# A hybrid decoder step: low-rank products kept in SBUF, four kinds of small work put elsewhere, and the last output tile taken whole

## The chip, the cores and the metric

The kernel runs on one core of a Trainium2 chip. The core has five engines with an instruction queue each: TensorE (PE in the profile; its weight loads are listed as PEld), VectorE (DVE), ScalarE (ACT), GpSimd (POOL) and SyncE (SP). Each takes its instructions in the order in which they were written to its queue; semaphores join the queues. Nearly all loads and stores are issued by SP. The metric is the time of one execution on the device, in microseconds (us), as the median of several runs.

## The reference

The step computes one layer for a prompt of 16 meta tokens and 1024 tokens, and for 8 samples of 4 new tokens each. A token has 2048 features. In short:

```python
h = rms_norm(x, norm_pre_g)
sq, sk, sv, sg, gq, gk, gv, gg, ga = split(h @ w_in)   # 8 x (1024 wide), ga is 16 wide
log_f = log_sigmoid(ga @ w_alpha + b_alpha) / 16       # decay of the gated linear attention
o_sb  = stick_breaking_attention(sq, sk, sv)           # 8 heads of 128; samples read paged keys and values
o_gla = gated_linear_attention(gq, gk, gv, log_f)      # 4 heads, key 128, value 256, state per sample
mixed = concat(o_sb * silu(sg), rms_norm(o_gla) * silu(gg))
y     = x + rms_norm(mixed @ w_out, norm_post_g)
```

`gq`, `gk` are 512 wide in all, `w_alpha` is 16 x 512. The outputs are y for prompt and samples, the new keys and values, and the final states. All data are float32. The kernel gets float32 accuracy from TensorE by splitting an operand into a rounded part and a rest, and by adding three products.

## The kernel before, in words

**Layout.** The normalized input is held transposed in SBUF, 16 tiles `hT0` to `hT15` of 128 features by 1072 tokens, each as a rounded part `hh` and a rest `hl`. A projection (`inproj`, L279) makes 128 output columns: eight weight blocks, each for three chunks of tokens (`CHUNKS`: 384, 384 and 304 columns), each chunk with two times three products (L289 to L291) into one of three PSUM banks (`acc`). After the last block each bank is emptied by an `evac` function on ACT.

**Weaving.** PE has most of the work, so everything else is woven in between. `Weaver` holds generators; `W.beat()` is called after each chunk of a weight block (six products) and advances them. `yield n` in a generator means: go on n beats later. So the beat is the unit in which small work is placed. The program text that results is then ordered for each engine by the framework's scheduler, which replays it on a model of the chip, takes the ready instruction that stands first in the text, and thereby fixes each queue's order. Parts marked `urgent()` are preferred. A "NoSync" dependency makes the scheduler put one instruction behind another on the queue and adds no wait on the chip.

**Stages, in order.** (1) Input, norm, transposes. (2) Eight attention heads: projections of v, k, q, and the attention itself woven in; at the same time DVE multiplies the paged keys of all samples with their queries (`z_feed`, L384), and pairs of `w_out` blocks are subtracted (`weight_forms`). (3) `low_rank` (L309): `ga` for all tokens, 32 rows (a rounded weight and a rest), 96 products. (4) Gate groups 0 to 2 (`gate_group`, L435): projection of 128 gate columns, then `gate_rest` (SiLU times the attention output, stored to DRAM as `md`). (5) Four linear-attention heads g: projections gk, gq, gv; the generator `decay` (L715) builds the running sums of log_f from `ga`; `inside` the products within a chunk; `chunks` the recurrence over nine chunks. (6) Gate groups 5 to 13, and the samples' attention over pages (`chain`, `new_keys`, `paged_values`). (7) Gate groups 14 and 15. (8) The output projection: seven products of half-size matrices (`forms` 1 to 7) instead of eight, whose sums make the four quadrants of the result; then norms and stores, tile by tile.

**What the change touches.**
`low_rank` writes its three row groups (rounded part, rest, rounded part again) through SBUF staging tiles to the DRAM tile `gad` with nine stores (L326). `decay` loads for each head a piece of `w_alpha` six times over 96 rows (`walr`, L719) and for each chunk of tokens a piece of `gad` (L725), makes `wal` from it on ACT (L730) and DVE (L731), and multiplies (L739).
`packed` (L852) transposes 96 columns, and `by_token` (L862) transposes whole 128-column blocks, both into the same PSUM bank (tag `tr`, one buffer), which ACT (L857, L872) and for `packed` also DVE (L859) empty. In `inside` the packed keys come first and then the three `by_token` groups; in `gv_tok` the packed values follow the last `by_token` at once.
`new_keys` (L1101) sums the new keys with a matmul (`Cs`, L1104) on beat 10 of stage 6. `chain` (L1115) loads stored logits (`dz`, L1121) and adds a bias 3 beats later (L1123).
`early` and `later` (L1221, L1227) load quarters of `md` and subtract or add them 2 beats later.
`form` (L1273) casts an operand into rounded part (ACT, L1263) and rest (DVE, L1264) in the memory of old `hT` tiles; form 2 is needed by the second product of the output projection.
At the end, four tiles t = 0 to 3 of 128 rows get their last product (form 4, weights `kept`, L1478 to L1480, 24 products of 512 columns); `take_last` adds, squares and scales, and `finish1` makes the norm's factor and stores. The last tile t = 3 is done in two halves of 256 columns.

## Time and profile before

| what | value |
| --- | --- |
| median of 3 runs | 2122.7 us (2122.02 to 2126.62) |
| the profiled execution | 2123.69 us, its span 2122.0 us |
| mean granted TensorE clock | 0.994 of full speed |
| PE, DVE, ACT, POOL busy | 97%, 74%, 47%, 4% of the span |
| DMA | 304 MB, mean 143 GB/s |

The span is the time from the first to the last instruction of the program. A row of a timeline has start, duration, engine, line, operation and "out<-in" by the program's names; what stands in square brackets is the idle time of the engine just before, and what ended it. A row of the list of waits has the waiting instruction, what it waited for, the total in us, how often, and the longest. A row of sums over a stretch has the busy time and number of instructions of each engine, then PEclk, the granted clock of TensorE as a share of full speed. In the tables below "PE b" is a product of the output projection, "acc" one of a projection, "gx" the emptying of a gate group's bank.

### The profile page before, as it was taken

What the parts mean: (1) busy time and instruction counts of PE and PEld (TensorE: products, weight loads), DVE (VectorE), ACT (ScalarE), POOL (GpSimd) and SP (SyncE); (2) the same over time, 40 slices, a digit from 0 to 9 for tenths busy, and PEclk for the clock granted to TensorE, in tenths of its full rate; (3) what the DMA queues carried; (4) which work ended last, traced back from release to release, by engine and by line L of the source; (5) the groups of instructions that cost most, each with busy time, mean ns of one, the idle gap of its engine ahead of it and who ended that gap; (6) DMA issues with size and microseconds to landing.
All of it is one profiled execution on the core that took longest, in us unless ns stands there. A gap on an engine that the chain in (4) does not pass through costs nothing.

```text
span 2122.0 us, 43405 instructions
## 1 busy us (share of the span) xinstructions
PE 2062.5 (97%) x12570; PEld 1874.1 (88%) x12570; DVE 1574.2 (74%) x6596; ACT 995.4 (47%) x2538; POOL 81.1 (4%) x298
## 2 busy tenths in 40 slices
PE   5999999999999999999999999999999999999997
PEld 4999999999999989999898998998888897777776
DVE  6368888889888889899798898977544446453575
ACT  7345556565555556434435335353444335342342
POOL 0000000100001000100000000000000000000000
PEclk9999999999999999999999999999999999999999
DMA  6244443544444454553443444335777665352484
GB/s 199 72 100 126 130 128 103 141 127 114 135 129 122 110 140 117 157 139 116 114 130 109 132 122 126 101 81 156 233 231 239 219 198 188 129 159 71 131 286 173
DMA packets 380586, 304.02 MB, mean 143 GB/s; under 512 B 50426, under 2 KB 320954, under 8 KB 380346
## 3 DMA queue, kind: packets, MB, share of 16 engines
q1 hardware_dynamic: 378154, 300.97, 48.2%
q8 instruction: 99, 1.62, 0.3%
q14 instruction: 141, 1.16, 0.2%
q10 hardware_dynamic: 2192, 0.27, 0.1%
HBM read 243.39 MB, written 57.72 MB: 142 GB/s over the span
## 4 chain that ended last, share of the span: by engine, by line
PE 79%; DVE 8%; DMA 8%; ACT 2%; issue 2%; SPq 1%; POOL 0%; DVEq 0%; ACTq 0%; POOLq 0%
PE acc_g L289 4%; PE b L1478 4%; PE acc_g L291 4%; PE acc_g L290 4%; PE b L1479 4%; PE b L1480 4%; PE acc_k L289 3%; PE acc_k L290 3%; PE acc_k L291 3%; PE acc_q L289 3%; PE acc_q L290 3%; PE acc_q L291 3%; PE acc_gv L289 3%; PE acc_v L289 3%; PE acc_gv L290 2%; PE acc_gv L291 2%
## 5 line engine op out<-in xcount | busy, mean ns | idle before, releaser
L384 DVE SCALAR_TENSOR_TENSOR jk<-kp,qb 128x128 f32<-128x128 f32 x2048 | 590.5, 288 | 39.6 <-DMA qb<-qsd 2.2
L289 PE MATMUL acc_g<-hT,wh_g 128*128 128x368 f32 (+2 forms) x768 | 251.5, 327 | 1.2 <-ACT gx L438 1.1
L291 PE MATMUL acc_g<-hT,wl_g 128*128 128x368 f32 (+2 forms) x768 | 248.1, 323 | 0.0
L290 PE MATMUL acc_g<-hT,wh_g 128*128 128x368 f32 (+2 forms) x768 | 247.6, 322 | 0.0
L1478 PE MATMUL b<-ring,f 128*128 128x512 f32 x416 | 166.2, 401 | 7.0 <-ACT gx L438 3.6
L1314 DVE TENSOR_TENSOR ring<-wr,ring 128x512 fp32r<-128x512 f32 x104 | 70.9, 690 | 133.2 <-ACT ring L1313 133.0
L384 DVE DVE_READ_ACCUMULATOR jk<-kp,qb 128x1 f32 x2048 | 165.9, 81 | 0.0
L1479 PE MATMUL b<-ring,f 128*128 128x512 f32 x416 | 162.9, 392 | 0.4 <-DVE ring L1314 0.4
L1480 PE MATMUL b<-ring,f 128*128 128x512 f32 x416 | 162.6, 391 | 0.0
L289 PEld LDWEIGHTS acc_g<-hT,wh_g 128*128 128x128 f32 x768 | 144.7, 188 | 12.9 <-issue 7.3
L291 PEld LDWEIGHTS acc_g<-hT,wl_g 128*128 128x128 f32 x768 | 144.8, 189 | 2.0 <-issue 2.0
L290 PEld LDWEIGHTS acc_g<-hT,wh_g 128*128 128x128 f32 x768 | 144.9, 189 | 0.7
L1313 ACT CAST ring<-wr 128x512 fp32r<-128x512 f32 x104 | 64.4, 621 | 163.1 <-DMA wr<-in_w_out_dram 76.2
L289 PE MATMUL acc_gv<-hT,wh_gv 128*128 128x384 f32 (+1 forms) x384 | 129.2, 337 | 0.0
L289 PE MATMUL acc_k<-hT,wh_k 128*128 128x378 f32 (+1 forms) x384 | 127.6, 332 | 0.0
L290 PE MATMUL acc_k<-hT,wh_k 128*128 128x378 f32 (+1 forms) x384 | 125.4, 326 | 0.0
L289 PE MATMUL acc_q<-hT,wh_q 128*128 128x368 f32 (+2 forms) x384 | 125.3, 326 | 0.0
L291 PE MATMUL acc_gv<-hT,wl_gv 128*128 128x384 f32 (+1 forms) x384 | 125.3, 326 | 0.0
L291 PE MATMUL acc_k<-hT,wl_k 128*128 128x378 f32 (+1 forms) x384 | 125.2, 326 | 0.0
L290 PE MATMUL acc_gv<-hT,wh_gv 128*128 128x384 f32 (+1 forms) x384 | 124.7, 325 | 0.0
L290 PE MATMUL acc_q<-hT,wh_q 128*128 128x368 f32 (+2 forms) x384 | 123.6, 322 | 0.0
L291 PE MATMUL acc_q<-hT,wl_q 128*128 128x368 f32 (+2 forms) x384 | 123.5, 322 | 0.0
(440 smaller groups left out, 5414.5 us busy)
## 6 DMA issues: line engine op xcount, KB each, us to landing
kp<-in_cache_k_dram SPq DMA_DIRECT2D x512, 64.0 KB
vr<-in_cache_v_dram SPq DMA_DIRECT2D x64, 512.0 KB
tf<-in_w_out_dram SPq DMA_DIRECT2D x64, 256.0 KB
qb<-qsd SPq DMA_DIRECT2D x64, 256.0 KB
td<-tf SPq DMA_DIRECT2D x64, 256.0 KB
wr_g<-in_w_in_dram SPq DMA_DIRECT2D x128, 128.0 KB
wr<-td SPq DMA_DIRECT2D x64, 256.0 KB
wr<-in_w_out_dram SPq DMA_DIRECT2D x48, 256.0 KB
```

What stands on the lines that cost most here:

```text
L289: mm(acc[c][:, :n], wh[:, k2, :], hh[k][:, lo:hi], start=(k == 0), stop=False)
L290: mm(acc[c][:, :n], wh[:, k2, :], hl[k][:, lo:hi], start=False, stop=False)
L291: W.mark = mm(acc[c][:, :n], wl[:, k2, :], hh[k][:, lo:hi], start=False, stop=(k == NK - 1)).ins
L384: ins = vec.scalar_tensor_tensor(jk[:], kp[:], 1.0, qbs[h, b][:, t, :], ALU.mult, ALU.mult, accum_out=zt[:, t, NPG - 1 - i:NPG - i])
L1313: act.copy(wh, r)
L1314: vec.tensor_tensor(wl, r, wh.bitcast(F32), ALU.subtract)
L1478: mm(bk[:, cs], ah, wh, start=first and k == 0, stop=False, skip_group_check=True)
L1479: mm(bk[:, cs], ah, wl, start=False, stop=False, skip_group_check=True)
L1480: mm(bk[:, cs], al, wh, start=False, stop=last and k == 7, skip_group_check=True)
```

## The change

- The low-rank products stay in SBUF: a tile `ga` of 96 rows by 1072 tokens takes the three row groups straight from PSUM (two ACT copies and one DVE subtraction for each chunk). All of `w_alpha` is loaded once (`walr`). The DRAM tile, its 9 stores, the 12 loads of `ga` and the 4 loads of `walr` go; one load of `walr` comes. `decay` has no `yield 6` at its start any more.
- `low_rank` goes over four k at a time for one chunk, so the three chunks end one after another.
- Packed keys are transposed one beat behind the last `by_token` group; packed values one beat behind theirs.
- `new_keys` starts on beat 14 in place of 10; `chain` adds its bias 6 beats behind its load in place of 3; `early` and `later` add 5 beats behind theirs in place of 2.
- The ACT casts of form 2 get a NoSync dependency on the last `gx` of gate group 15.
- The last tile is done whole, as the other three.

```diff
+    ga = dk.tile([96, T], F32R, tag="ga", bufs=1, name="ga")
+    walr = dk.tile([96, GH * P], F32, tag="walr", bufs=1, name="walr")
     def low_rank_weights():
+        a = w_alpha[0]
+        nc.sync.dma_start(walr[:], bass.AP(tensor=a.tensor, offset=a.offset, ap=[[0, 6]] + [list(d) for d in a.ap]))
...
-        for k in range(NK):
+        for kb in range(0, NK, 4):
             for c, (lo, hi) in enumerate(CHUNKS):
                 n = hi - lo
-                mm(acc[c][:32, :n], wa[k // 8][:, k % 8, :], hh[k][:, lo:hi], start=(k == 0), stop=False)
-                mm(acc[c][:32, :n], wa[k // 8][:, k % 8, :], hl[k][:, lo:hi], start=False, stop=(k == NK - 1))
+                for k in range(kb, kb + 4):
+                    mm(acc[c][:32, :n], wa[k // 8][:, k % 8, :], hh[k][:, lo:hi], start=(k == 0), stop=False)
+                    mm(acc[c][:32, :n], wa[k // 8][:, k % 8, :], hl[k][:, lo:hi], start=False, stop=(k == NK - 1))
+                W.beat()
             W.beat()
...
-                act.copy(hi_[:, :n], acc[c][:32, :n])
-                vec.tensor_tensor(lo_[:, :n], acc[c][:32, :n], hi_[:, :n].bitcast(F32), ALU.subtract)
-                for i, t in enumerate((hi_, lo_, hi_)):
-                    nc.sync.dma_start(gad[32 * i:32 * i + 32, lo:hi], t[:, :n].bitcast(F32))
+                ps = acc[c][:32, :hi - lo]
+                act.copy(ga[0:32, lo:hi], ps)
+                act.copy(ga[64:96, lo:hi], ps)
+                vec.tensor_tensor(ga[32:64, lo:hi], ps, ga[0:32, lo:hi].bitcast(F32), ALU.subtract)
...
+    evacs = []
     def gate_group(g):
         def evac(c, ps, lo, hi):
             x = stage(f"gx{g}_{c}")
-            act.copy(x[:, :hi - lo], ps)
+            evacs.append(act.copy(x[:, :hi - lo], ps).ins)
...
         def decay(g, cb):
-            raw = stage(f"walr{g}")[:96, :P]
...
-            load_ga(0)
-            yield 6
+            gs = slice(g * P, (g + 1) * P)
+            raw = walr[:, gs]
             wal = gp.tile([96, P], F32R, tag="wal", name=f"wal{g}")
...
-                mm(ps[:, :n], wal[:], ga[:, :n], start=True, stop=True)
+                mm(ps[:, :n], wal[:], ga[:, lo:hi], start=True, stop=True)
...
-            packed(rep_, pk[:], 2, f"k{g}")
             by_token(kt, kd, (0, 4), col, f"k{g}")
             yield 1
             by_token(kt, kd, (4, 4), col, f"k{g}")
             yield 1
             by_token(kt, kd, (8, 1), col, f"k{g}")
             res["kd"], res["ebl"], res["pk"] = kd, ebl, pk
+            yield 1
+            packed(rep_, pk[:], 2, f"k{g}")
...
             if c == 2:
+                yield 1
                 packed(rep, pv[:, f * P:(f + 1) * P], 1, f"v{g}_{f}")
...
         def new_keys():
-            yield 10
+            yield 14
...
             nc.sync.dma_start(z[:].rearrange("p a r -> p (a r)"), zd[b][:])
-            yield 3
+            yield 6
...
         def early(k):
-            yield 2
+            yield 5
         def later(k):
-            yield 2
+            yield 5
...
-        def split(hi, lo, src):
-            act.copy(hi, src)
+        def split(hi, lo, src, behind=None):
+            ins = act.copy(hi, src)
+            if behind is not None:
+                tc.add_manual_dep(ins.ins, behind.name, NOSYNC, reason="behind")
...
-                    split(f[:, 0], f[:, 1], combined(p, k))
+                    split(f[:, 0], f[:, 1], combined(p, k), evacs[-1] if p == 2 else None)
...
         for t in range(4):
             tot = before_last(t)
-            w = 256 if t == 3 else 512
-            for f in range(512 // w):
-                for k in range(8):
-                    product(banks[t], t, 4, k, kept[k], False, True, slice(f * w, (f + 1) * w))
-                    W.beat()
-                take_last(t, banks[t], tot, f, w)
-            finish1(t, tot[:, 512 // w:512 // w + 1])
+            for k in range(8):
+                product(banks[t], t, 4, k, kept[k], False, True)
+                W.beat()
+            take_last(t, banks[t], tot)
+            finish1(t, tot[:, 1:2])
```

`finish1` itself is not edited: it still forms the last output of tile 3 in two halves of 256 columns, each with its own store.

More of the change, by code (lines that the diff above doesn't have):

```diff
@@ L151, in hybrid_step @@
     znd = dram.tile([NSMP, HEADS, NSMP], F32, name="znd")
-    gad = dram.tile([96, T], F32, name="gad")
     td = [dram.tile([P, 8, 1024], F32, name=f"td{j}") for j in range(4)]
@@ L295, in inproj @@
                 W.beat()
+    dk_cm = tc.tile_pool(name="dk", bufs=2, side="right")
+    dk = dk_cm.__enter__()
     wa = []
+    ga = dk.tile([96, T], F32R, tag="ga", bufs=1, name="ga")
+    walr = dk.tile([96, GH * P], F32, tag="walr", bufs=1, name="walr")
     def low_rank_weights():
+        a = w_alpha[0]
+        nc.sync.dma_start(walr[:], bass.AP(tensor=a.tensor, offset=a.offset, ap=[[0, 6]] + [list(d) for d in a.ap]))
         war = stage("war")
@@ L319, in low_rank @@
             with urgent():
-                n = hi - lo
-                hi_ = stg.tile([32, 384], F32R, tag="stg", name=f"gah{c}")
-                lo_ = stg.tile([32, 384], F32R, tag="stg", name=f"gal{c}")
-                act.copy(hi_[:, :n], acc[c][:32, :n])
-                vec.tensor_tensor(lo_[:, :n], acc[c][:32, :n], hi_[:, :n].bitcast(F32), ALU.subtract)
-                for i, t in enumerate((hi_, lo_, hi_)):
-                    nc.sync.dma_start(gad[32 * i:32 * i + 32, lo:hi], t[:, :n].bitcast(F32))
-    dk_cm = tc.tile_pool(name="dk", bufs=2, side="right")
-    dk = dk_cm.__enter__()
+                ps = acc[c][:32, :hi - lo]
+                act.copy(ga[0:32, lo:hi], ps)
+                act.copy(ga[64:96, lo:hi], ps)
+                vec.tensor_tensor(ga[32:64, lo:hi], ps, ga[0:32, lo:hi].bitcast(F32), ALU.subtract)
     paged = {}
@@ L715, in decay @@
         def decay(g, cb):
-            raw = stage(f"walr{g}")[:96, :P]
-            a = w_alpha[0, :, g * P:(g + 1) * P]
-            nc.sync.dma_start(raw, bass.AP(tensor=a.tensor, offset=a.offset, ap=[[0, 6]] + [list(d) for d in a.ap]))
-            gas = {}
-            def load_ga(c):
-                lo, hi = CHUNKS[c]
-                gas[c] = stg.tile([96, 384], F32R, tag="stg", name=f"ga{g}_{c}")
-                nc.sync.dma_start(gas[c][:, :hi - lo].bitcast(F32), gad[:, lo:hi])
-            load_ga(0)
-            yield 6
+            gs = slice(g * P, (g + 1) * P)
+            raw = walr[:, gs]
             wal = gp.tile([96, P], F32R, tag="wal", name=f"wal{g}")
@@ L734, in decay @@
                 yield 5
-                ga = gas.pop(c)
-                if c < 2:
-                    load_ga(c + 1)
                 ps = gps.tile([P, 512], F32, tag="P", bufs=2, name=f"al{g}_{c}")
-                mm(ps[:, :n], wal[:], ga[:, :n], start=True, stop=True)
+                mm(ps[:, :n], wal[:], ga[:, lo:hi], start=True, stop=True)
                 ny = stage(f"ny{g}_{c}")[:, :n]
@@ L1387, in before_last, with take_last @@
             return tot
-        def take_last(t, bk, tot, f, w):
-            cs = slice(f * w, (f + 1) * w)
+        def take_last(t, bk, tot):
             u = sums_[4 + t, 1]
-            if f == 0:
-                scaled[t] = raw(f"og{t}")
+            scaled[t] = raw(f"og{t}")
             with urgent():
-                vec.tensor_tensor(u[:, cs], bk[:, cs], u[:, cs], ALU.add)
-            part = ssq[:, 4 + t, 2 + f:3 + f]
-            act.activation(bk[:, cs], u[:, cs], AF.Square, accum_out=part)
-            vec.tensor_tensor(scaled[t][:, cs], u[:, cs], gains[1][:, cs], ALU.mult)
-            vec.scalar_tensor_tensor(tot[:, f + 1:f + 2], part, 1.0 / D, tot[:, f:f + 1], ALU.mult, ALU.add)
+                vec.tensor_tensor(u, bk[:], u, ALU.add)
+            part = ssq[:, 4 + t, 2:3]
+            act.activation(bk[:], u, AF.Square, accum_out=part)
+            vec.tensor_tensor(scaled[t][:], u, gains[1][:], ALU.mult)
+            vec.scalar_tensor_tensor(tot[:, 1:2], part, 1.0 / D, tot[:, 0:1], ALU.mult, ALU.add)
         def sample_y(sc, b):
@@ L1473, in finish1, with product @@
                     nc.sync.dma_start(y_prompt[0, 512 + i * P:512 + (i + 1) * P, ys], o[:, cs])
-        def product(bk, t, p, k, w, first, last, cs=slice(0, 512)):
-            wh, wl = (x[:, cs] for x in w)
+        def product(bk, t, p, k, w, first, last):
+            wh, wl = w
             ah, al = (forms[p, k][:, s_, t * P:(t + 1) * P] for s_ in range(2))
-            mm(bk[:, cs], ah, wh, start=first and k == 0, stop=False, skip_group_check=True)
-            mm(bk[:, cs], ah, wl, start=False, stop=False, skip_group_check=True)
-            mm(bk[:, cs], al, wh, start=False, stop=last and k == 7, skip_group_check=True)
+            mm(bk[:], ah, wh, start=first and k == 0, stop=False, skip_group_check=True)
+            mm(bk[:], ah, wl, start=False, stop=False, skip_group_check=True)
+            mm(bk[:], al, wh, start=False, stop=last and k == 7, skip_group_check=True)
         SB = {}
```

## The prediction

> **What bounds the kernel now.** I read the page's busy times first, then the list of what PE waited for, then sums over stretches behind those waits, and last the timelines around each wait that the change can touch.

> ```profile
> PE 2062.5 (97%) x12570; PEld 1874.1 (88%) x12570; DVE 1574.2 (74%) x6596; ACT 995.4 (47%) x2538; POOL 81.1 (4%) x298
> ```

> PE is busy for 97% of a span of 2122.0 us. The change takes no product away, so a gain can only come out of PE's idle time and out of what that idle time does to its clock. The list of waits says where that is (total, times, longest):

> ```profile
> PE al L739 <- DMA ga<-gad: 4.1, 2, 2.8
> PE b L1478 <- ACT gx L438: 3.6, 1, 3.6
> PE trp_v L856 <- ACT gv L872: 3.3, 3, 2.3
> PE Cs L1104 <- issue: 2.9, 1, 2.9
> PE tr_k L867 <- DVE pk L859: 2.2, 3, 0.7
> PE b L1478 <- ACT b L1398: 2.2, 1, 2.2
> PE acc_ga L315 <- DVE q L621: 1.6, 2, 1.5
> PE acc_g L289 <- ACT gx L438: 1.1, 1, 1.1
> PE otr L891 <- ACT gst L893: 0.7, 3, 0.2
> PE trp_k L856 <- DVE rep_k L850: 0.4, 1, 0.4
> ```

> Those of 2.2 us and more are each near an edit; the waits of the start, which no edit touches, are left out. What they cost beyond their length is in the granted clock (the eighth figure is PEclk) of the stretches behind them, in the order al, a later al, trp_v, Cs, b after gx, b after L1398:

> ```profile
> 896.00:900.00 4.00, 4.00 (x15) 4.00 (x16) 3.79 (x25) 1.61 (x3) 4.00 (x16) 0.60 0.39 112
> 911.00:915.00 4.00, 3.96 (x24) 3.96 (x25) 3.69 (x25) 1.54 (x6) 0.00 (x0) 1.00 0.56 175
> 1134.60:1140.00 5.40, 5.37 (x28) 5.38 (x29) 3.17 (x23) 2.32 (x8) 0.00 (x0) 0.68 0.32 97
> 1485.70:1491.00 5.30, 5.25 (x22) 4.65 (x23) 3.61 (x9) 2.16 (x5) 0.00 (x0) 0.68 0.65 226
> 1771.00:1775.00 4.00, 4.00 (x12) 3.14 (x13) 3.81 (x11) 4.00 (x10) 0.00 (x0) 0.62 0.17 30
> 2109.00:2113.00 4.00, 4.00 (x23) 4.00 (x24) 1.61 (x4) 0.00 (x0) 0.00 (x0) 0.63 0.62 240
> ```

> Each wait of 2.2 us or more is followed by a slow stretch; the second al wait (4.1 - 2.8 = 1.3 us) is not. A slow stretch loses (1 - PEclk) x length: 1.6, 1.7, 1.7, 1.5 and 1.5 us.
> [...] The rows show it after 2.2 us already, so I count it.

> **The change, part by part.**

> *Low-rank products in SBUF.* Both al waits go, since `ga` needs no load: 4.1 + 1.6 = 5.7 us. The 25 DMAs that go and the one that comes are issued by SP between waits and cost PE nothing. `walr` has an effect on another wait:

> ```profile
> 1133.54 0.30 ACT L730 CAST wal<-walr 96x128 fp32r<-96x128 f32 x1 [2.61 <-DMA walr<-in_w_alpha_dram]
> 1134.63 0.31 PE L856 MATMUL trp_v<-ident,rep_v 128*96 128x128 f32 x1 [2.25 <-ACT gv L872]
> ```

> ACT stands 2.61 us at the cast of `wal`, and behind it on its queue stands the copy that frees the transposes' bank; PE's 2.25 us at trp_v is the wait for that copy. With `walr` resident the cast waits for nothing, so the 3.3 us of trp_v go with this part, whatever the beat of `packed` is: 3.3 + 1.7 = 5.0 us. What is late next there is the copy itself, which the scheduler has counted.

> *Extra evacuation work and order in `low_rank`.* Three more ACT copies.

> ```profile
> 794.64 0.84 ACT L323 CAST gah<-acc_ga 32x384 fp32r<-32x384 f32 x2 [1.25 <-PE acc_ga L316]
> ```

> Two take 0.84 us, so three cost 1.3 us of an ACT that stood idle 1.25 us there; the first two chunks now end 16 and 8 products earlier and cover it. The 1.5 us wait at the start of `low_rank` is for the bank of chunk 0, needed first in both orders: it stays; the other 0.1 us goes. I take 0, ends -1.3 and +0.1. `decay` starts 6 beats earlier and so still meets the chunk recurrence: three otr waits of 0.2 us stand beside al products now; if all 9 al products of heads 1 to 3 met one, that would cost 9 x 0.2 = 1.8 less the 0.7 there. I take -0.5.

> *Transposes sharing a bank.*

> ```profile
> 992.35 0.66 PE L867 MATMUL tr_k<-ident,gk 128*128 128x128 f32 x4 [0.74 <-DVE pk L859]
> ```

> The packed keys hold the bank through an ACT and then a DVE step (pk), and the next user waits 0.74 us for it. With the packed keys last, that goes for tr_k (2.2 + 0.4 = 2.6 us at most), but the value transposes use the same bank in the same beats, and one of them will stand behind pk. The end +2.6 is no follower waiting, 0 the same wait moved, -2.6 the wait doubled. Nearest is the moved wait with a beat between: +1.0.

> *Key sums; bias; first forms' sums.* Between the start of gate group 5 and Cs, and up to a later load of `dz`, the projections' products are:

> ```profile
> 1464.00:1485.70 21.70, 18.75 (x116) 18.45 (x116) 0.39 (x1) 1.00 0.56 163
> 1464.00:1534.50 70.50, 60.55 (x360) 58.27 (x360) 3.05 (x7) 0.98 0.68 215
> 1534.55 0.34 SPq L1121 DMA_DIRECT2D dz<-zd  x1
> 1482.52 0.42 DVE L1123 TENSOR_TENSOR dz<-dz,bias 128x256 f32<-128x256 f32 x1 [1.53 <-DMA dz<-zd]
> 1485.25 0.41 DVE L1086 TENSOR_TENSOR spb<-spn,bmask 32x256 f32<-32x256 f32 x1
> ```

> A beat is six products, so Cs stands 116 / 6 = 19.3 beats in, while the text has it on beat 10: what placed it was its operand `spb`, ready in the scheduler's model only then. Beat 14 is ahead of 19.3 too. And the load of `dz` for batch 3 stands on beat 60, twelve ahead of its place in the text (72): work off PE runs as soon as it is ready, whatever its beat. So I expect nothing from 10 to 14, 3 to 6 and 2 to 5: 0. The upper end is the whole wait, 2.9 + 1.7 = 4.6 us; the lower, that the 1.1 us wait at gate group 15 (its ACT work stands behind DVE sums that wait for loads) doubles: -1.1.

> *Casts of form 2 behind gate 15.*

> ```profile
> 1763.91 0.62 ACT L1263 CAST f<-q 128x512 fp32r<-128x512 f32 x1 [2.43 <-DMA q<-md]
> 1766.98 0.30 PE L291 MATMUL acc_g<-hT,wl_g 128*128 128x304 f32 x1
> 1770.33 0.46 ACT L438 COPY gx<-acc_g 128x368 f32<-128x368 f32 x1
> 1772.12 0.40 ACT L438 COPY gx<-acc_g 128x304 f32<-128x304 f32 x1
> ```

> Eleven casts, six f<-q (form 2) and five f<-s (form 6), run on ACT from 1763.91 to 1770.33, 0.58 us apart, ahead of the gx that PE waits for. Only the f<-q are put behind. If the five others start at 1763.91 they end at 1763.91 + 5 x 0.58 = 1766.8, and gx at 1767.3, when PE's last product (1766.98 + 0.30) ends: 3.6 + 1.5 = 5.1 us go. Late next are the weights of blocks 6 and 7:

> ```profile
> 1784.80 1.54 SPq L1204 DMA_DIRECT2D small<-md  x1
> 1786.91 0.86 SPq L1312 DMA_DIRECT2D wr<-in_w_out_dram  x2
> 1791.71 0.50 PE L1478 MATMUL b<-ring,f 128*128 128x512 f32 x1 [0.62 <-ACT ring L1313]
> ```

> SP holds that load behind `small`, which reads gate 15's last store; that chain starts with the last gx, which moves from 1772.12 to the end of the products, some 1767.7: 4.4 us, where PE moves 5.1. So this wait grows by 0.7 us. The eight casts of form 2 now lie beside the gate's own work on ACT; one in its way costs 0.6. I take 5.1 - 0.7 - 0.6 = 3.8, ends 0 and 5.1.

> *Last tile whole.*

> ```profile
> 2098.18 0.39 PE L1478 MATMUL b<-keep,f 128*128 128x512 f32 x1
> 2103.62 0.28 PE L1478 MATMUL b<-keep,f 128*128 128x256 f32 x1
> 2104.36 0.68 DVE L1396 TENSOR_TENSOR u<-b,u 128x512 f32<-128x512 f32 x1
> 2107.14 0.75 DVE L1472 SCALAR_TENSOR_TENSOR u<-u,r_y,xrs 128x512 f32<-128x512 f32 x1
> 2116.38 1.41 DVE L1472 SCALAR_TENSOR_TENSOR y<-y,r_y,xr 128x512 f32<-128x512 f32 x2
> 2117.70 0.87 DVE L1472 SCALAR_TENSOR_TENSOR og<-og,r_y,xrs 128x256 f32<-128x256 f32 x2
> ```

> A whole tile takes 2103.62 - 2098.18 = 5.4 us, so the last ends at 2109.2. DVE gives tile 2's four outputs, two in 1.4 us, until 2107.14 + 2.7 = 2109.8, then adds; from add to first output 2.8 us (2107.14 - 2104.36), so 2112.6; the outputs take 2.9 (0.75 less overlap, 1.4, 0.87), so 2115.5; from there to the end of the span 2122.0 - 2118.6 = 3.4: 2118.9. Gain 3.1 us. The half tiles' overlap, which is given up, is in that count. Ends 1.0 (all longer steps twice in a row) and 3.8 (the add goes ahead of one 0.7 us output).

> **Sum.** 5.7 + 5.0 + 0 - 0.5 + 1.0 + 0 + 3.8 + 3.1 = 18.1 us, against the profiled execution's 2123.7 (span 2122.0): 2105.6. Its own time is 1.0 above the runs' median of 2122.7, so the median comes to 2104.6; I say 2105.

> **The rivals.**
> (a) *The key sums' wait goes too* (if DVE no longer stands 1.53 us at `dz` ahead of `spb`): 2105 - 4.6 = 2100.
> (b) *The weight blocks take back what form 2 gave.* A wait at a pair of blocks that reaches 2.2 us brings a slow stretch: 2.2 - 0.6 + 1.6 = 3.2 us a pair; at two pairs, with the 0.7 counted already, 2105 + 5.7 = 2111. For it: the wait is there (0.62) and grows; against: 0.7 more isn't 2.2.
> (c) *Slow stretches stay though waits go*, because something else than these waits sets them: 1.6 + 1.7 + 1.5 back, 2110. Against it: five of five waits of 2.2 us or more have one and the 1.3 us wait has none. [...]
> (d) *New order, same idle time.* The scheduler lays every queue anew; fresh waits as large as those removed: 2122.
> (e) *Slower:* SP starves the output projection. The second form's loads wait for buffers that its casts free, and the casts stand behind gx; if SP holds weight loads behind them, each pair of blocks costs 2.2 + 1.6 = 3.8 us. The rest gains 14.3, so four pairs even out; at five it is 2122.7 - 14.3 + 19 = 2127. Against it:

> ```profile
> SPq L1312 <- PE sc L1498: 8.9, 3, 6.2
> ```

> SP's weight loads wait for PE's own last reading of the old block, so they come earlier when PE does.

> **How the numbers follow.** Forecast 0.58, (a) 0.14, (b) 0.11, (c) 0.06, (d) 0.05, (e) 0.06. The range takes in (a), (b) and (c), and beside them some 2 us for the bank's ends: 2098 to 2113. Within 0.2% (4.2 us, about what a measurement can tell from no change) only (d): 0.05; slower (e) 0.06; faster 0.89.

> **What would show it.** No al, trp_v or b-after-L1398 wait and no half clock at those places; no ACT idle before `wal`; gx of gate 15 ending near PE's last product; Cs still waiting about 2.9 us with a slow stretch; a DVE wait before a transpose of values. Wrong: a Cs wait much longer (PE ahead of DVE), or waits over 2 us at L1478 in the first steps.

## The result, and the profile after

The changed kernel takes 2112.4 us (median of six runs, 2108.2 to 2114.1) where the kernel before takes 2122.8: a ratio of 0.9947, 95% interval 0.9934 to 0.9959, or 11.3 us (8.7 to 14.0) less. The forecast was 2105, its range 2098 to 2113, so the result is inside by 0.6 us. The profiled execution of the changed kernel took 2108.2 us, its span is 2106.5; it is the shortest of the six. The profile page has for it:

```profile
PE 2056.2 (98%) x12546; PEld 1868.4 (89%) x12546; DVE 1569.7 (75%) x6593; ACT 991.8 (47%) x2539; POOL 80.9 (4%) x298
```

PE is still the bound, with 24 products fewer because the last tile is no longer computed in two halves. The list of what PE waited for (line and what was waited for, then total, times, longest, in us; the start is left out):

```profile
PE Cs L1097 <- issue: 2.3, 1, 2.3
PE acc_gq L288 <- ACT gk L673: 2.2, 1, 2.2
PE b L1471 <- ACT b L1344: 2.0, 2, 1.2
PE acc_gk L288 <- ACT gx L442: 1.8, 1, 1.8
PE Us L961 <- DVE km L958: 1.5, 1, 1.5
PE acc_ga L321 <- DVE q L625: 1.3, 1, 1.3
PE acc_gq L288 <- ACT gk L680: 1.2, 1, 1.2
PE b L1471 <- ACT gx L442: 1.2, 1, 1.2
PE acc_g L288 <- ACT gx L442: 0.8, 1, 0.8
...
PE tr_v L859 <- DVE pk L851: 0.7, 1, 0.7
```

`al`, `trp_v`, `tr_k` and the 2.2 us wait for the first half of the last tile (b on L1398) are gone; one `tr_v` wait of 0.7 us behind `pk` has come, as forecast. The b wait for gx fell from 3.6 to 1.2, Cs kept 2.3. What no step of the forecast had are acc_gk, acc_gq (two) and Us: 1.8 + 2.2 + 1.2 + 1.5 = 6.7 us of new waits.

For all kernels below I added up PE's gaps of over 0.1 us between products from the trace, by stretch, and the time lost to half clock (half the length of those stretches up to PE's last product, since the granted clock is 0.50 in them; those after the last product cost nothing and are left out; the wait ahead of the first b product counts with the output projection):

| kernel | span | 870 to 1000 (first head) | 1000 to the last gv | last gv to 1495 | 1495 to first b | output projection | half clock |
|---|---|---|---|---|---|---|---|
| before | 2122.0 | 5.5 | 5.6 | 3.4 | 1.4 | 9.7 | 10.2 |
| changed | 2106.5 | 5.1 | 2.0 | 3.9 | 1.1 | 4.0 | 6.8 |
| changed, second trace | 2111.9 | 6.5 | 1.9 | 4.6 | 1.2 | 4.1 | 6.8 |

The second trace (an execution of 2113.6 us, near the median) is the one to set beside the kernel before: 10.1 us less span. The output projection gave 5.6, the heads after the first 3.7, the half clock 3.4; the first head gave nothing (+1.0) and the stretch up to Cs took 1.2 back. The end behind PE's last product is 0.9 us longer in both. Of the half clock, 3.4 us in the changed kernel's first trace and 1.7 in the other two lie ahead of 60 us; past 60 us it costs 8.5, 3.4 and 5.1 us in the three rows.

### The profile page after: what moved, and what is told of

Read it like the earlier page. It is cut to its first block, busy times and chain, and to the rows that moved or that the text cites. A ratio compares the mean times of both kernels' runs of the same rounds, so it can differ in the third digit from the quotient of the medians.

```text
span 2106.5 us, 43298 instructions
## 1 busy us (share of the span) xinstructions
PE 2056.2 (98%) x12546; PEld 1868.4 (89%) x12546; DVE 1569.7 (75%) x6593; ACT 991.8 (47%) x2539; POOL 80.9 (4%) x298
## 3 DMA queue, kind: packets, MB, share of 16 engines
q14 instruction: 142, 1.16, 0.2%
## 4 chain that ended last, share of the span: by engine, by line
PE 84%; DMA 6%; DVE 6%; ACT 2%; issue 1%; SPq 0%; DVEq 0%; POOL 0%; ACTq 0%; POOLq 0%
PE acc_g L288 4%; PE acc_g L290 4%; PE b L1471 4%; PE acc_g L289 4%; PE b L1472 4%; PE b L1473 4%; PE acc_k L288 3%; PE acc_gv L288 3%; PE acc_k L289 3%; PE acc_q L288 3%; PE acc_k L290 3%; PE acc_gv L290 3%; PE acc_gv L289 3%; PE acc_q L289 3%; PE acc_q L290 3%; PE acc_v L288 3%
## 5 line engine op out<-in xcount | busy, mean ns | idle before, releaser
L289 PE MATMUL acc_g<-hT,wh_g 128*128 128x368 f32 (+2 forms) x768 | 247.9, 323 | 0.0
L1472 PE MATMUL b<-ring,f 128*128 128x512 f32 x416 | 162.8, 391 | 0.7 <-DVE ring L1309 0.5
L288 PEld LDWEIGHTS acc_g<-hT,wh_g 128*128 128x128 f32 x768 | 145.1, 189 | 12.4 <-issue 10.2
L289 PEld LDWEIGHTS acc_g<-hT,wh_g 128*128 128x128 f32 x768 | 145.1, 189 | 0.7
L289 PE MATMUL acc_k<-hT,wh_k 128*128 128x378 f32 (+1 forms) x384 | 125.5, 327 | 0.0
L289 PE MATMUL acc_gv<-hT,wh_gv 128*128 128x384 f32 (+1 forms) x384 | 124.6, 325 | 0.0
L289 PE MATMUL acc_q<-hT,wh_q 128*128 128x368 f32 (+2 forms) x384 | 123.8, 322 | 0.0
```

The lines of the kernel that those rows point to most:

```text
L288: mm(acc[c][:, :n], wh[:, k2, :], hh[k][:, lo:hi], start=(k == 0), stop=False)
L289: mm(acc[c][:, :n], wh[:, k2, :], hl[k][:, lo:hi], start=False, stop=False)
L1472: mm(bk[:], ah, wl, start=False, stop=False, skip_group_check=True)
```

## The experiments

Each time below is set against runs of the kernel before that were made beside it on the same chip, as a ratio with its 95% interval; the microseconds are 1 less that ratio, times the median of those runs. Those medians differ (2126.4, 2122.7 and 2124.7 in three series of runs), so only ratios are compared from one series to another.

### One part at a time

**The low-rank part alone** (`lowrank`): `ga` and `walr` in SBUF, the sums in runs of four blocks, `decay` without loads and lag.

```diff
-            raw = stage(f"walr{g}")[:96, :P]
...
-            yield 6
+            gs = slice(g * P, (g + 1) * P)
+            raw = walr[:, gs]
...
-                mm(ps[:, :n], wal[:], ga[:, :n], start=True, stop=True)
+                mm(ps[:, :n], wal[:], ga[:, lo:hi], start=True, stop=True)
```

> The kernel before with the low-rank part alone: ga and walr in SBUF, the sums over 32 blocks in runs of four, decay without its loads and without its lag of six beats. The forecast's terms 5.7 + 5.0 - 0.5 give 10.2 us less than before, some 2112.6, with no al and no trp_v wait. Rival (earlier decay blocks ACT): in the changed kernel's trace PE waits 1.76 us for gx at the first acc_gk product and 2.16 + 1.19 us for gk at acc_gq, with a slow stretch of 1.7 us after them, because ACT stood 5.2 us at an exponential of the decay that now comes earlier; if the low-rank part makes these, they stand in this trace too and the gain is 10.2 - 6.3 = 4 us, some 2119.

Ratio 0.9981 (0.9970 to 0.9992): 4.0 us less (1.7 to 6.4). That is the rival's number; its cause, the earlier `decay`, is a part of it only, as the next kernel shows. PE's waits between 870 and 1000 us in this kernel:

```profile
PE acc_gq L288 <- ACT gk L678: 2.5, 1, 2.5
PE acc_gk L288 <- ACT gx L440: 2.4, 1, 2.4
PE acc_gq L288 <- ACT gk L671: 1.3, 1, 1.3
PE tr_k L856 <- DVE pk L848: 0.7, 1, 0.7
```

The two al waits are gone and three waits of 6.2 us in all stand in their place. So the new waits belong to this part and not to the others.

**Only `walr` resident** (`walr`); gad, its loads and the lag stay.

```diff
-            raw = stage(f"walr{g}")[:96, :P]
-            a = w_alpha[0, :, g * P:(g + 1) * P]
-            nc.sync.dma_start(raw, bass.AP(tensor=a.tensor, offset=a.offset, ap=[[0, 6]] + [list(d) for d in a.ap]))
+            raw = walr[:, g * P:(g + 1) * P]
```

> The kernel before with walr resident in SBUF alone; gad and its loads and the lag of six beats stay. The forecast takes the trp_v waits to be those of an ACT queue that stands at the wal cast for its load: then 3.3 + 1.7 = 5.0 us go, some 2117.7, and the al waits on ga stay at 4.1. Rival (the trp_v waits come from something else in the order of the queue, and went in the changed kernel by the transposes' new order): 2122.7, with trp_v still waiting.

Ratio 0.9992 (0.9982 to 1.0003): 1.7 us less (0.6 more to 3.8 less), so the 5.0 lie outside. In the same stretch:

```profile
PE acc_gk L289 <- ACT gx L441: 2.1, 1, 2.1
PE al L740 <- DMA ga<-gad: 1.8, 1, 1.8
PE al L740 <- DMA wr_gk<-in_w_in_dram: 0.8, 1, 0.8
...
PE trp_v L857 <- ACT gv L873: 0.4, 1, 0.4
```

Of 3.3 us of trp_v 0.4 is left, although `packed` stands where it stood: those waits were the `wal` cast's load, as argued. But acc_gk appears with this edit alone: it is in each of the seven traces with `walr` resident and the gates' order unchanged, and in none of the five without `walr`.

**The transposes' order alone** (`transp`), the two `yield 1` and `packed` last.

```diff
-            packed(rep_, pk[:], 2, f"k{g}")
...
             res["kd"], res["ebl"], res["pk"] = kd, ebl, pk
+            yield 1
+            packed(rep_, pk[:], 2, f"k{g}")
...
```

> The kernel before with the order of the transposes alone: the packed ones behind those by token. The forecast: 1.0 us less (ends: 2.6 less and 2.6 more), with the three tr_k waits of 0.74 us gone and a wait at a value transpose in their place. Rival (the trp_v wait of 2.25 us with its slow stretch moves too, since the packed value transposes now come a beat later): 3.9 us more go, 2118 or less. In the changed kernel's trace one tr_v wait of 0.69 us is left.

Ratio 0.9988 (0.9977 to 0.9998): 2.5 us less (0.4 to 4.9). The tr_k waits are gone; trp_v has three waits of 3.8 us in all, the longest 1.5, where before it had 3.3 with one of 2.25. The idle time of the heads after the first is 5.6 us in both traces; what is gone there is the half clock at 1135.7 (a granted clock of 0.51 from 1135.7 to 1139.1 us), which stood behind a single wait of 2.25 us and doesn't stand behind the three shorter ones. This is one trace of each; elsewhere in it, too, half clock is absent at places that the edit does not touch.

**The four yields alone** (`yields`).

```diff
-            yield 10
+            yield 14
...
```

> The kernel before with the four changed yields alone (10 to 14, 3 to 6, 2 to 5 twice). The forecast: 0 us, the wait at Cs stays at 2.9 us with its slow stretch (in the changed kernel 2.34 us and a slow stretch, after the same 19.3 beats). Rival: the page sums' later places make DVE free ahead of the key sums, Cs waits 1 us less and the stretch goes: 2.7 us less, 2120.

Ratio 0.9998 (0.9987 to 1.0009): nothing. Cs waits 3.0 us and is followed by half clock.

**Form 2's casts alone** (`casts`).

```diff
-                    split(f[:, 0], f[:, 1], combined(p, k))
+                    split(f[:, 0], f[:, 1], combined(p, k), evacs[-1] if p == 2 else None)
...
```

> The kernel before with form 2's casts behind gate 15's last gx alone. The forecast: 3.8 us less, some 2119, the weight blocks' wait of 0.62 us grows to about 1.3. Rival 1 (only the wait that the changed kernel's trace shows gone, 3.55 to 1.16, and no slow stretch): 2.4 + 1.5 = 3.9 and the ring waits of 0.62 + 0.22 go too: 4.7, some 2118. Rival 2 (SP holds weight loads behind the form's own loads): new waits above 1 us at the first weight blocks, 2122 or more.

Ratio 0.9986 (0.9977 to 0.9996): 3.0 us less (0.9 to 4.9). What is left of the wait is seen in the changed kernel's timelines of ACT and PE (start, length, what ran, idle time before it and what ended it):

```profile
1757.42 0.46 ACT L442 COPY gx<-acc_g 128x368 f32<-128x368 f32 x1
1758.30 0.48 ACT L442 COPY gx<-acc_g 128x384 f32<-128x384 f32 x1 [0.42 <-PE acc_g L290]
1760.38 0.92 ACT L427 ACTIVATE gs<-gs 128x368 f32<-128x368 f32 x2 [1.60 <-DVE gs L426]
1761.21 0.39 ACT L442 COPY gx<-acc_g 128x304 f32<-128x304 f32 x1
1761.66 0.49 PE L1471 MATMUL b<-ring,f 128*128 128x512 f32 x1 [1.16 <-ACT gx L442]
```

No cast stands ahead of the last gx any more. The gate's own exponential does, and it waits 1.60 us for DVE; PE waits 1.16 for the copy behind it. That is the same form of wait as at acc_gk. In the trace of `casts` itself, the slowest of its runs (2127.8 us), the exponential waits 2.50 us for DVE and PE 2.06, with half clock behind it. The seven traces of the changed kernel and of those made from it below wait 0.6 to 1.3 us there; without the edit it is anything from 1.0 (`transp`) to 3.7 (`yields`). So what the edit saves at this place is seen only roughly.

**The last tile alone** (`last`).

```diff
-                for k in range(8):
-                    product(banks[t], t, 4, k, kept[k], False, True, slice(f * w, (f + 1) * w))
+            for k in range(8):
+                product(banks[t], t, 4, k, kept[k], False, True)
...
```

> The kernel before with the last tile whole alone. The forecast: 3.1 us less, some 2119.6; PE ends 2.2 + 1.7 us earlier and the tail after PE's last product grows by about 0.8. Rival (the tail takes it back, because the add of 512 columns and its outputs stand behind four outputs of tile 2 on DVE): tail grows by 2.9, gain 1.0, some 2121.7.

Ratio 0.9982 (0.9973 to 0.9991): 3.8 us less (1.9 to 5.7). The changed kernel's DVE shows the chain that was costed:

```profile
2092.05 0.68 DVE L1389 TENSOR_TENSOR u<-b,u 128x512 f32<-128x512 f32 x1
2097.49 0.68 DVE L1389 TENSOR_TENSOR u<-b,u 128x512 f32<-128x512 f32 x1
2102.25 0.88 DVE L1465 SCALAR_TENSOR_TENSOR og<-og,r_y,xrs 128x256 f32<-128x256 f32 x2
2096.50 0.39 PE L1473 MATMUL b<-keep,f 128*128 128x512 f32 x1
```

The add of the last tile starts 0.6 us after PE's last product has ended (2097.49 against 2096.50 + 0.39), right behind tile 2's outputs, and the tail after PE grows from 8.7 to 9.6 us.

The five parts sum to 4.0 + 2.5 + 0.4 + 3.0 + 3.8 = 13.7 us, against 11.3 and, in the run below, 12.5 for the whole. They add up within their intervals; the shortfall against 18.1 sits in the low-rank part, 4.0 for 10.2.

### The changed kernel once more

> The changed kernel once more. Its first six runs lie between 2108.2 and 2114.1, those of the kernel before between 2122.0 and 2123.0 but for one. Theory 1 (clock): a gap on PE near the length at which the clock is halved goes one way or the other from run to run; then a slower run's trace shows one to three more slow stretches of 1.7 us, or other gaps at the same places. Theory 2 (a transfer that lands at another time): the same slow stretches, but a wait that is longer by some us at a place that hangs on a transfer. A run near 2112 would settle it; one near 2108 looks like the trace at hand.

2113.6 us, ratio 0.9941 (0.9926 to 0.9957). The trace is the second one in the table: nearly the same waits at the same places, those at acc_gk, acc_gq and Cs each 0.6 to 0.8 us longer (acc_gk 2.4, acc_gq 2.9, Cs 3.0), and after Cs two windows of half clock where the first trace has one. Its span is 5.4 us longer: PE idles 3.6 us more in all and is busy 1.9 us longer, about what one window of half clock costs. So both theories hold in part: waits differ by some tenths from run to run, and half clock adds a step of 1.7 us.

### Where the first head's gain went

PE's two waits there have one form: on ACT the copy that PE waits for stands behind an exponential, and that stands at a step of DVE. First acc_gk in the changed kernel (DVE, ACT, ACT, PE):

```profile
882.06 0.34 DVE L426 TENSOR_SCALAR gs<-gx 128x368 f32<-128x368 f32 x1
882.44 0.51 ACT L427 ACTIVATE gs<-gs 128x368 f32<-128x368 f32 x1 [3.23 <-DVE gs L426]
882.86 0.46 ACT L442 COPY gx<-acc_g 128x384 f32<-128x384 f32 x1
883.37 0.44 PE L288 MATMUL acc_gk<-hT,wh_gk 128*128 128x384 f32 x1 [1.76 <-ACT gx L442]
```

Then ACT, DVE and PE where the first head's keys end:

```profile
900.90 0.51 ACT L733 ACTIVATE ny<-al,nbal 128x304 f32<-128x304 f32 x1
906.79 0.46 ACT L735 ACTIVATE e<-e 128x304 f32<-128x304 f32 x1 [5.20 <-issue]
908.20 0.27 ACT L673 COPY gk<-acc_gk 128x128 f32<-128x128 f32 x1
906.20 0.51 DVE L734 TENSOR_SCALAR e<-ny 128x304 f32<-128x304 f32 x1
908.52 0.45 PE L288 MATMUL acc_gq<-hT,wh_gq 128*128 128x384 f32 x1 [2.16 <-ACT gk L673]
```

`ny` of the third chunk is there at 901.4. DVE takes its clamp (L734) only at 906.20, behind key products and other steps; ACT stands 5.20 us at the exponential behind the clamp; the gk copies, whose products ended at 906.4, stand behind the exponential; PE waits 2.16 us for them. Before, the third al product stood at its load until 911, so that its exponential came behind the gk copies.

**The lag put back** (`after_lag`), `yield 6` ahead of the `wal` cast.

```diff
             raw = walr[:, gs]
+            yield 6
             wal = gp.tile([96, P], F32R, tag="wal", name=f"wal{g}")
```

> The changed kernel with the lag of six beats put back at the head of decay, ahead of the wal cast. If the earlier decay is what makes PE wait for gk at acc_gq (2.16 + 1.19 us and a slow stretch of 1.7 us), these go and the kernel is 5 us faster than the changed one, some 2107 against 2112. If the lag does nothing because ACT takes the cast as soon as it is ready in either case, the time is the changed kernel's within 1 us, with the same waits.

Ratio 0.9952 (0.9939 to 0.9966), the changed kernel's within the intervals, and acc_gq waits 3.5 us. Now the second chunk's exponential stands ahead of the gk copies, as it did before the change. First its row in this kernel, then the one in the kernel before:

```profile
908.30 0.52 ACT L736 ACTIVATE e<-e 128x384 f32<-128x384 f32 x1 [5.92 <-DVE e L735]
```

```profile
905.98 0.53 ACT L744 ACTIVATE e<-e 128x384 f32<-128x384 f32 x1 [1.43 <-DVE e L743]
```

In the same order ACT waits 5.92 us for DVE instead of 1.43. So it is not only the order on ACT: DVE itself is late, and it was so at acc_gk already, ahead of every al product. From the end of the first gx copy of that gate to DVE's step on it the kernels without resident `walr` (before, `transp`, `yields`, `casts`, `last`) take 0.2 to 0.5 us, and those with it 2.3 to 3.1 (3.9 and 4.4 in the two with the gates' exponentials moved). DVE loses the time here, in the changed kernel:

```profile
869.04 0.30 ACT L724 CAST wal<-walr 96x128 fp32r<-96x128 f32 x1 [4.67 <-DMA od<-ost]
869.37 0.28 DVE L725 TENSOR_TENSOR wal<-walr,wal 32x128 fp32r<-32x128 f32 x1 [2.54 <-ACT wal L724]
```

and in the kernel before:

```profile
893.88 0.28 DVE L731 TENSOR_TENSOR wal<-walr,wal 32x128 fp32r<-32x128 f32 x1 [0.79 <-ACT wal L730]
```

With no load to wait for, the cast of the first head's `wal` is laid 24 us earlier, into a stretch where ACT stands 4.67 us at it until a store (od<-ost) has ended, and DVE stands 2.54 us at the low part behind it. All seven traces above have that DVE wait, 2.5 to 2.7 us; without resident `walr` it is 0.8 to 1.2, and later. In the two kernels with the gates' exponentials moved it is 0.4 and 0.6, but there DVE stands 2.5 and 1.9 us at a load (go<-od) just ahead. In the 45 us ahead of the first acc_gk product DVE idles 5.1 to 6.2 us in the nine traces with resident `walr` and 3.2 to 3.6 in the five without, and it has done 1159 to 1162 key products by then, not 1166 or 1167. PE has products to run at that time and doesn't notice. DVE, busy 56.2 us of the next 60 (the third figure, from 880 on), cannot make it up:

```profile
880.00:940.00 60.00, 54.89 (x332) 53.82 (x331) 56.20 (x287) 22.55 (x57) 11.78 (x35) 0.97 0.53 147
```

So PE pays at the first places where it hangs on DVE through ACT: acc_gk 14 us later and acc_gq 40 us later. That chain is read from the traces and not shown by an edit; a kernel that only ties the cast to a later product, so that DVE doesn't stand there, would prove it and was not tried. The lag of six beats could not do it: it is a place in the text, and the cast, which is not on PE, starts when its operands are there (869.3 with the lag, 869.0 without).

**The third chunk put ten beats later** (`after_gk`).

```diff
-                yield 5
+                yield 15 if (g, c) == (0, 2) else 5
```

> The changed kernel with the third part of the first head's decay ten beats later (yield 15 in place of 5 there). Theory (the decay that no longer waits for a load puts an exponential ahead of ACT's copies of gk, and that exponential stands behind DVE's key products): in ACT's queue the gk copies now come first, so the waits at acc_gq (2.16 + 1.19 us and 2.94 + 1.01 us in two traces of the changed kernel, 3.52 with the lag) go, and with them a slow stretch of 1.7: 5 us, some 2108 where the changed kernel has 2112 to 2113. Rival (ACT is late at gk for another reason, as the kernel with the lag, which kept the wait, could also mean): acc_gq still waits over 2 us, time unchanged.

Ratio 0.9958 (0.9943 to 0.9972): not faster than the changed kernel. PE's waits between 870 and 1000 us:

```profile
PE trp_v L848 <- ACT gv L864: 2.9, 1, 2.9
PE acc_gq L290 <- DVE wl_gq L184: 2.3, 1, 2.3
PE acc_gk L288 <- ACT gx L442: 2.0, 1, 2.0
PE acc_gv L288 <- ACT gq L992: 0.7, 1, 0.7
```

The wait for gk is gone. Two products later PE waits 2.3 us for DVE itself, and at 971.8 another 2.9 us for a copy on ACT. What DVE did meanwhile:

```profile
908.72 0.23 DVE L711 CAST lvl<-lv 128x128 uint8<-128x128 f32 x1 [1.78 <-POOL lv L708]
909.41 0.42 DVE L184 TENSOR_TENSOR wl_gq<-wr_gq,wh_gq 128x256 fp32r<-128x256 f32 x1
```

It stood 1.78 us at a level mask from POOL that its queue had ahead of the weights' low part. This stretch idles 8.0 us, more than in any other trace: the order on ACT was mended, and DVE's lateness stayed.

**The gates' exponentials behind their copies** (`after_behind`).

```diff
-        act.activation(s, s, AF.Exp)
+        ins = act.activation(s, s, AF.Exp).ins
+        tc.add_manual_dep(ins, evacs[-1].name, NOSYNC, reason="behind")
...
-            W.spawn(gate_rest(g, lo, hi, x), 1)
+            W.spawn(gate_rest(g, lo, hi, x), 3 - c)
```

> The changed kernel with each gate's first exponential put behind the gate's three gx copies on ACT. The same theory at the first acc_gk product: there PE waits 1.76 and 2.38 us, because the copy of the second chunk stands behind the exponential of the first, which stands at DVE. The wait at acc_gk goes, that at the first b product (1.16, 0.75) and at acc_g (0.8) shrink: 2 to 3 us, or 4 where the wait brought a slow stretch, some 2109.5. Rival (DVE is late for the copies as well, or the later exponentials make the gates' stores late): waits move to another product, gain under 1 us.

Ratio 0.9983 (0.9974 to 0.9991): some 8 us slower than the changed kernel. The acc_gk wait for gx is gone, as the theory has it, and others came: acc_gq 2.9 and 1.8, a load of a state (os, 2.5), a weight cast (acc_g, 1.7), the ring (3.7 in four). Postponing ACT's share of all gates costs more than the one wait is worth; which of those it caused and which came with the new order of the queues, these runs don't separate.

**The key sums later** (`after_keys`).

```diff
-            yield 14
+            yield 23
...
-            yield 8
+            yield 8 if b else 14
```

> The changed kernel with the key sums at beat 23 in place of 14 and the first page's sums 6 beats later. Theory (the yield of 14 does nothing since the product stands at 19.3 beats for its operand's sake; PE gets there 2.3 to 3.0 us ahead of DVE): at some 24 beats, 28 products of 0.167 us or 4.7 us later, the operand is there, the wait of 2.34 to 2.98 us goes and a slow stretch of 1.7 to 3.4 us with it: 4 to 6 us, some 2107.5. Rival (DVE's work on the first page slides along and Cs waits as before): unchanged.

The product starts 4.7 us later in PE's order and finds its operand:

```profile
1482.24 0.41 DVE L1079 TENSOR_TENSOR spb<-spn,bmask 32x256 f32<-32x256 f32 x1
1484.18 0.69 PE L1097 MATMUL Cs<-spb,nones 32*128 32x256 f32 x2
```

No wait and no half clock there. Yet the ratio is 0.9943 (0.9929 to 0.9958), the changed kernel's 0.9941 and 0.9947. In its trace the first head's waits are there and were followed by half clock twice, an oT wait of 1.4 us came, and acc_g waits 2.5 us for gx in four pieces. A saving of 4 us was in the trace at its place; the whole time doesn't show it.

**All three edits** (`best`).

> The changed kernel with all three edits. If the three waits are independent, 5 + 3 + 5 us go: some 2100, where the changed kernel has 2112 to 2113 and the one before 2123 to 2126. Rival (DVE is as much behind as PE, and the waits come back at the next place that needs DVE): 2107 or more.

Ratio 0.9968 (0.9955 to 0.9980): some 5 us slower than the changed kernel, though the intervals overlap a little. The three waits are gone (acc_gq for gk, acc_gk for gx, Cs); acc_gq waits 2.9 us for DVE, trp_v 2.8, os 2.8. No kernel here beats the changed one.

The first head's idle time in all fourteen traces lies between 4.7 and 8.0 us, whatever was taken away or moved in it.

### What a wait costs in clock

The starts of half clock within one trace differ by whole multiples of 3.413 us: before the change 896.8, 1135.7, 1487.3, 1770.6 and 2108.5 are 70, 103, 83 and 99 of them apart, and in the first trace of the changed kernel 909.2 and 1479.2 are 167. The grid lies elsewhere in each trace; from 896.8 to 909.2 it is 3.6 steps. Cut along that grid, with PE's busy time as the first figure and the granted clock as the eighth:

```profile
891.00:894.40 3.40, 1.93 (x13) 1.69 (x11) 2.27 (x11) 0.66 (x3) 0.00 (x0) 1.00 0.66 197
894.40:897.80 3.40, 1.66 (x10) 1.69 (x11) 3.21 (x18) 0.83 (x2) 3.25 (x11) 1.00 0.72 205
897.80:901.20 3.40, 3.40 (x22) 3.40 (x22) 3.34 (x20) 1.34 (x3) 3.40 (x12) 1.00 0.29 71
908.10:911.50 3.40, 1.45 (x9) 1.20 (x9) 3.30 (x17) 1.67 (x7) 0.00 (x0) 1.00 0.83 258
911.50:914.90 3.40, 3.40 (x14) 3.40 (x13) 3.16 (x22) 0.46 (x1) 0.00 (x0) 0.50 0.52 161
```

These are of `transp`. Its al wait of 3.2 us lies across two windows, 1.5 and 1.7 us in each, and nothing follows; its wait of 1.95 us lies within one, and the next window runs at 0.50. In the kernel before, the windows ahead of those five starts have 2.57, 2.25, 1.86, 3.32 and 1.85 us of idle PE, and the next ones run at 0.50 or 0.51; the changed kernel's two have 2.16 each. In `walr` a window with 1.76 us idle was followed by one at 0.50 and another with 1.76 by one at 1.00; in `casts` one with 1.89 was followed by one at 1.00. Counted over the fourteen traces, from 60 us to PE's last product, each of the 29 windows with 1.95 us or more of idle PE was followed by half clock, of those with 1.76 to 1.94 some were and some not, and below that, of windows at full clock, only four at Cs were (1.1 to 1.6 us idle; why Cs differs, these traces don't show). Of windows that themselves ran at half clock, all five with 0.9 to 1.2 us of idle PE were followed by another.

## Why the prediction was right, and where it failed

The sign and most terms held; the result lies at the upper end of the range, 7 us above the forecast. That the range reached so far was luck in part: its upper end was drawn for rivals (b) and (c), and what raised the time was neither, but new waits in the first head. The opening statement that the change takes no product away is not exact: the last tile's 48 products of 256 columns become 24 of 512. Point by point:

- *Low-rank products in SBUF, 5.7 us for al.* Failed. The al waits went, but the stretch from 870 to 1000 us idles 5.1 and 6.5 us where it idled 5.5. Two steps failed. "With `walr` resident the cast waits for nothing": in the first head it waits 4.67 us for a store, and DVE 2.54 behind it. And the other: the 0.5 us set down for `decay` starting earlier were costed where an al product meets the chunk recurrence in the later heads, not in the first, where an exponential then stands ahead of the gk copies. Measured in their place: 3.4 to 4.0 us at acc_gq and 1.8 to 2.4 at acc_gk, with half clock behind one or two of them. The text itself said under the yields that work off PE runs as soon as it is ready, and did not apply it to this cast.
- *trp_v, 5.0 us.* The reason was right: with `walr` resident alone, 0.4 of 3.3 us is left. The same edit brought acc_gk, and alone it measured 1.7 (-0.6 to 3.8).
- *Extra work in `low_rank`, 0.* Right: acc_ga waits 1.3 and 2.1 us, where the kernels without this part have 1.5 to 2.1.
- *Transposes, 1.0.* The wait moved to tr_v, as forecast. Measured 2.5, within the ends; in the one trace the heads idle no less, and the difference lies in the clock.
- *Yields, 0.* Right, and for the reason given: Cs stands 116 products in with 14 as with 10, and moved when the yield was past that point (144 products with 23). Rival (a) didn't come.
- *Form 2's casts, 3.8.* 3.0, a little less: the gate's own exponential holds the last gx. The weights of blocks 6 and 7, which were to make PE wait 0.7 us longer, do not do so in the traces of the changed kernel and of `casts` (0.1 us at most). Rivals (b) and (e) didn't come.
- *Last tile, 3.1.* 3.8 (1.9 to 5.7), by the chain that was costed.
- *The slow stretches, 6.3 us (1.6, 1.7 and 1.5 in the sum, 1.5 within the last tile's).* All four that were to go are gone. But new ones came, one behind acc_gq in both traces and a second behind Cs in one: past 60 us half clock fell by 5.1 and 3.4 us. And the step "Each wait of 2.2 us or more is followed by a slow stretch" held in the one trace that the forecast had and is not certain: of the five traces that wait 2.3 to 3.2 us at al, two have half clock there, and of the six that wait 2.2 us or more at the last tile's first half, four. An estimate from the traces' steps of 3.41 us, and from 1.85 us of idle PE in one window as the middle of the 1.76 to 1.94 at which some windows were followed by half clock: a wait of length w between 1.85 and 3.7 us is followed by it with the chance 1 - (3.7 - w) / 3.41, 0.56 at 2.2 us and 0.77 at 2.9. 1.7 us times such chances (0.73, 0.57, 0.96 and 0.55 for the waits of 2.77, 2.25, 3.55 and 2.16) is an estimate of 4.8 us, and the new waits give some of it back. Rival (c), that the stretches stay, did not come.
- *Rival (d), new waits as large as those removed, at 0.05.* For the kernel as a whole it didn't come; in the first head it is what happened, and in the kernels made to mend it (`after_lag`, `after_gk`, `after_behind`, `best`) it came again.

## What to carry to other kernels

A load that is taken away lets the work behind it be laid earlier, here the first `wal` cast by 24 us: ask for each instruction that hung on it where it will stand then, what it will find there, and what stands behind it on its queue. The 2.5 us that DVE lost at that cast's low part, ahead of 60 us in which it was busy for 56.2, turned up, as the traces read, in waits of PE 14 and 40 us later, at places that have nothing to do with the edit; mending those places one by one only moved the waits. A cost that comes in steps, as the half clock does with 1.7 us here, goes into a sum with a chance and not as certain.
